# The opening of a pooling mixer, rebuilt: the scale row spread by TensorE, another load order, whole float32 weights for two tiles

## The chip, the cores and the metric

The kernel runs on one core of a Trainium2 chip. The metric is the device time of one execution in microseconds (us), as the median of several runs. The core has five engines, each with an instruction stream of its own that it works through in order: TensorE (PE, matrix products), VectorE (DVE), ScalarE (ACT), GpSimd (POOL) and SyncE (SP, which issues most DMAs). They wait for each other through semaphores.

## The reference: what is computed

One layer of a decoder trunk on x of 1024 tokens by 1024 channels, float32. The first half is the pooling mixer, the second a gated ConvFFN:

```python
h = rms_norm(x, norm_mix_g)
# per group of 256 channels, windows (2, 4, 8, 16):
d = causal_window_mean(h, w) - h
y = scale * (einsum('bsgc,gcd->bsgd', d, w) + b)
x = x + y
f = conv_ffn(rms_norm(x, norm_ffn_g))   # 1024 -> 2*2816, conv of 3, silu(gate)*val, 2816 -> 1024
x = x + f
```

`rms_norm` multiplies by the gain and by 1/sqrt(mean(x*x) + 1e-6).

## The kernel before, in words

The tokens are cut into eight tiles of 128 rows, `xs[0]` to `xs[7]`. A loop over j runs a software pipeline in which tile j is normed, tile j-1 is pooled, tile j-2 is multiplied by the mixer's weights and tile j-4 becomes an operand of the FFN. The steps of a tile:

- `rstd_of` (L127 to L138): ACT sums the squares of a tile (`junk`, L130) and takes a square root (L131); DVE then makes the reciprocal root from it with five operations on one column (`st`, L132 to L137). There is one such norm per tile ahead of the mixer (`st_a`), one ahead of the FFN (`st_b`), and one for `x_edge` (`st_e`).
- `mixer_norm` (L145): DVE multiplies the band matrix of the four windows by each row's reciprocal root (`bandr`, L147). The pooling is a matmul of the tile with that matrix, so the norm costs nothing more.
- `mixer_window` (L188): PE makes the pooled tile `psd` with eight float32 matmuls of 128 columns (L151; a record each for two halves, so x16 in the trace). DVE corrects the first 16 columns of each chunk: for tile 0 by a factor (L196), for the others by adding `edges`, what the window takes from the tile before (L198). ACT rounds the result to `dh` (L199), DVE makes the rest `dl` (L200).
- `mixer_edges` (L166): `x_edge` holds the last 16 rows of each of the first seven tiles (rows 16 to 127 of it). It has a norm of its own and an `edge_band`; PE makes `ps_edges` for all tiles at once, ACT copies it to `edges` (L169).
- `mixer_weights` (L175): DVE multiplies the weights `wp_raw` by the scale row, spread over 128 partitions, and by the norm's gain (L178); ACT rounds them to `wph` (L183), DVE makes the rest `wpl` (L184).
- `mixer_bias` (L157): the bias row, spread over 128 partitions too, times the scale, split in two parts for a matmul with a constant matrix (L159 to L162, L215).
- `mixer_out` (L206): PE multiplies, per chunk, dh*wph + dh*wpl + dl*wph, 24 matmuls of 256 columns (`psy`, L214), and two of 512 columns for the bias (L215). DVE adds the tile itself (L217), SP stores it (L218), and the second norm follows (`diag`, L221).
- `ffn_operand` (L233): PE transposes and norms the tile (`pst`, L237), ACT and DVE scale it into `n2f` and split it into operands of the FFN's matmuls.

The FFN (L263 to the end) is a Strassen-like scheme of three-term matmuls (L303, L576) whose weights come in as `win` tiles of 1 MB. Its first two, `win0` and `win1`, are loaded inside the mixer's loop, into the two buffers of the tag "raw" that `wp_raw` and `rows_b` (scale and bias rows) have held.

The order on each engine is fixed when the program is built: a scheduler places the instructions from the order of the code and from what they depend on, and `tc.issue_after(mark)` holds a group of instructions back behind a marked one. On an engine nothing overtakes. All loads of the opening are issued by SP, in the order of L108 to L119.

Of the kernel before, what the change touches and what calls it, by code (L numbers as in the profile page):

```python
# [7 lines left out]
F32 = mybir.dt.float32  # L8
F32R = mybir.dt.float32r
# [12 lines left out]
NG = 4  # L22
# [11 lines left out]
BD = B0 + NG * P  # L34

NOPS_A = 3
ACT_GAIN = 7

NH = 512
# [4 lines left out]
def trunk_kernel(ctx: ExitStack, tc: tile.TileContext, x, consts, par, rows, pool_w, w_in, w_out, out):  # L44
# [16 lines left out]
    def raw_tile(name):  # L61
        return work.tile([P, 2, D], F32, tag="raw", name=name, bufs=2)
# [24 lines left out]
    def affine(t, src, op, fill, base, pattern, step):  # L87
        nc.gpsimd.affine_select(out=t, in_=src, compare_op=op, fill=fill, base=base, pattern=pattern, channel_multiplier=step)

    nc.gpsimd.memset(x_edge[:HALO, :], 0.0)  # L90
    for g, w in enumerate(WINDOWS):

        e = edge_band[:, g, :].rearrange("p (j t) -> p j t", t=HALO)
        nc.gpsimd.memset(edge_band[:, g, :], 1.0 / w)
        affine(e, e, ALU.is_gt, 0.0, w - HALO, [[-HALO, NS], [-1, HALO]], 1)
        affine(e, e, ALU.is_ge, 0.0, HALO - 1, [[HALO, NS], [0, HALO]], -1)
    for g, w in enumerate(WINDOWS):

        m = band[:, g, :]
        nc.gpsimd.memset(m, 1.0 / w)  # L100
        affine(m, m, ALU.is_ge, 0.0, 0, [[1, P]], -1)
        affine(m, m, ALU.is_gt, 0.0, w, [[-1, P]], 1)
        affine(m, m, ALU.not_equal, 1.0 / w - 1.0, 0, [[1, P]], -1)
    par_sb = const.tile([P, NPAR], F32, tag="par", name="par_sb")
    wp_raw = raw_tile("wp_raw").rearrange("p a (c d) -> p (a c) d", d=GRP)
    rows_b = raw_tile("rows_b")
    scale_b, bias_b = rows_b[:, 0, :], rows_b[:, 1, :]
    load_x(0)  # L108
    nc.sync.dma_start(cst, consts)
    nc.sync.dma_start(x_edge[HALO:, :], x.rearrange("(j r) d -> j r d", r=P)[: NS - 1, P - HALO :, :])  # L110
    nc.sync.dma_start(par_sb, par)
    nc.sync.dma_start(scale_b, rows[:1, :].to_broadcast([P, D]))
    load_x(1)
    for g in range(0, NG, 2):
        nc.sync.dma_start(wp_raw[:, 2 * g : 2 * g + 4, :], pool_w[g : g + 2].rearrange("g (k p) d -> p (g k) d", p=P))
# [6 lines left out]
    nc.vector.memset(eps_t, EPS)  # L122
# [4 lines left out]
    def rstd_of(src, name):  # L127
        junk = pp.tile([P, D], BF16, tag="junk", name=f"junk_{name}")
        st = pp.tile([P, 4], F32, tag="st", name=f"st_{name}", bufs=8)
        nc.scalar.activation(junk, src, AF.Square, accum_out=st[:, 0:1])  # L130
        nc.scalar.activation(st[:, 1:2], st[:, 0:1], AF.Sqrt, bias=eps_t, scale=1.0 / D)  # L131
        nc.vector.tensor_scalar(st[:, 0:1], st[:, 0:1], 1.0 / D, EPS, op0=ALU.mult, op1=ALU.add)  # L132
        nc.vector.reciprocal(st[:, 2:3], st[:, 1:2])

        nc.vector.scalar_tensor_tensor(st[:, 3:4], st[:, 2:3], st[:, 0:1], st[:, 2:3], op0=ALU.mult, op1=ALU.mult)
        nc.vector.tensor_scalar(st[:, 3:4], st[:, 3:4], -0.5, 1.5, op0=ALU.mult, op1=ALU.add)
        nc.vector.tensor_tensor(st[:, 2:3], st[:, 2:3], st[:, 3:4], ALU.mult)  # L137
        return st[:, 2:3]  # L138

    bands, marks, stats = {}, {}, {}  # L140

    def edge_norm():
        nc.vector.tensor_scalar(edge_band, edge_band, rstd_of(x_edge, "e"), None, op0=ALU.mult)

    def mixer_norm(j):  # L145
        t = bands[j] = pp.tile([P, NG, P], F32, tag="bandr", name=f"bandr{j}", bufs=2)
        nc.vector.tensor_scalar(t, band if j else band0, stats[j], None, op0=ALU.mult)  # L147

    def windows(ps, src, weights):
        for c in range(NK):  # L150
            nc.tensor.matmul(ps[:, c * P : (c + 1) * P], src[:, c * P : (c + 1) * P], weights[:, c // 2, :], start=True, stop=True)  # L151


    bias_hl = pp.tile([P, D], F32R, tag="bias_hl", name="bias_hl")
    mean_w = pp.tile([P, P], F32R, tag="mean_w", name="mean_w")

    def mixer_bias():  # L157
        nc.vector.memset(mean_w.bitcast(F32), 2.0 / P)
        nc.vector.tensor_tensor(bias_b, bias_b, scale_b, ALU.mult)  # L159
        nc.scalar.activation(bias_hl, bias_b, AF.Copy)  # L160
        low = slice(P // 2, P)
        nc.vector.tensor_tensor(bias_hl[low, :], bias_b[low, :], bias_hl[low, :].bitcast(F32), ALU.subtract)  # L162

    edges = pp.tile([P, NK, P], F32, tag="edges", name="edges")

# [9 lines left out]
    def mixer_weights():  # L175
        for c in range(2 * NG):
            g = c // 2
            nc.vector.scalar_tensor_tensor(  # L178
                wp_raw[:, c, :], scale_b[:, g * GRP : (g + 1) * GRP], par_sb[:, GM + c : GM + c + 1], wp_raw[:, c, :], op0=ALU.mult, op1=ALU.mult
            )  # L180
            if c % 2:
                cs = slice(c - 1, c + 1)
                nc.scalar.activation(wph[:, cs, :], wp_raw[:, cs, :], AF.Copy)  # L183
                nc.vector.tensor_tensor(wpl[:, cs, :], wp_raw[:, cs, :], wph[:, cs, :].bitcast(F32), ALU.subtract)  # L184

    ds = {}

    def mixer_window(j):  # L188
        ps = bank2(f"psd{j}")
        windows(ps, xs[j], bands.pop(j))  # L190
        dh = pp.tile([P, NK, P], F32R, tag="dh", name=f"dh{j}", bufs=2)
        dl = pp.tile([P, NK, P], F32R, tag="dl", name=f"dl{j}", bufs=1)
        ps3 = ps.rearrange("p (c s) -> p c s", c=NK)
        first = ps3[:, :, :HALO]
        if j == 0:
            nc.vector.tensor_tensor(first, first, fac, ALU.mult)  # L196
        else:
            nc.vector.tensor_tensor(first, first, edges[:, :, j * HALO : (j + 1) * HALO], ALU.add)  # L198
        nc.scalar.activation(dh, ps3, AF.Copy)  # L199
        nc.vector.tensor_tensor(dl, ps3, dh.bitcast(F32), ALU.subtract)  # L200
        ds[j] = (dh, dl)

    n2s = {}
    x1_dram = dram.tile([S, D], F32, tag="x1_dram", name="x1_dram")

    def mixer_out(j):  # L206
        dh, dl = ds.pop(j)
        ps = bank2(f"psy{j}")
        for h in range(2):
            cols = slice(h * NH, (h + 1) * NH)  # L210
            for c in range(4 * h, 4 * h + 4):
                o = ps[:, c // 2 * GRP : (c // 2 + 1) * GRP]
                for i, (a, w) in enumerate(((dh, wph), (dh, wpl), (dl, wph))):
                    nc.tensor.matmul(o, a[:, c, :], w[:, c, :], start=c % 4 == 0 and i == 0, stop=False, skip_group_check=True)  # L214
            nc.tensor.matmul(ps[:, cols], mean_w, bias_hl[:, cols], start=False, stop=True, skip_group_check=True)  # L215
        x1 = xs.pop(j)
        marks[j] = nc.vector.tensor_tensor(x1, ps, x1, ALU.add).ins  # L217
# [3 lines left out]
        nc.vector.tensor_scalar(diag, ident, r, None, op0=ALU.mult)  # L221
        n2s[j] = (x1, diag)

    n2f = n2_pool.tile([P, NK, S], F32, tag="n2f", name="n2f")
# [164 lines left out]
    for j in range(NS + 4):  # L389
        if j < NS:  # L390
            mixer_norm(j)
        if j == 0:
            edge_norm()
            stat(1)
        if 0 <= j - 1 < NS:
            mixer_window(j - 1)
        if j == 1:
            mixer_edges()
            mixer_weights()
            mixer_bias()  # L400
# [12 lines left out]
        stat(j + 1)  # L413
# [191 lines left out]
def constants():  # L605

    import numpy as np

    r, t, h = np.arange(P)[:, None], np.arange(P), np.arange(HALO)
    blocks = [np.eye(P)]  # L610
    blocks += [np.tile(w / np.minimum(h + 1, w), (P, 2)) for w in WINDOWS]
    inside = [(r > t - w) & (r <= t) for w in WINDOWS]
    blocks += [(m - np.eye(P) * np.minimum(t + 1, w)) / w for m, w in zip(inside, WINDOWS)]
    return np.concatenate(blocks, axis=1).astype(np.float32)


# [32 lines left out]
```

## Time and profile before

| what | value |
|---|---|
| median of 3 runs | 720.9 us (719.9 to 721.37) |
| the profiled execution | 723.45 us |
| its span, first to last instruction | 721.7 us |
| granted TensorE clock over the span | 0.995 |
| PE busy | 698.9 us (97%) |
| DVE busy | 609.7 us (84%) |
| ACT busy | 352.3 us (49%) |

All rows of the trace are of the profiled execution, counted from the start of its span. A timeline row reads: start, duration, engine, line, operation, what it writes <- what it reads, partitions x elements, count, and in brackets the idle time just before it with what ended it. In a table of windows each engine has its busy time in the stretch with the number of instructions; then come the granted clock (1.00 is full), the DMA engines' busy share and the bytes they moved per second. SPq marks the issue of a DMA by SP: its duration is the time to issue, not to transfer.

### The profile page before, as it was taken

What the parts mean: (1) busy time and instruction counts of PE and PEld (TensorE: products, weight loads), DVE (VectorE), ACT (ScalarE), POOL (GpSimd) and SP (SyncE); (2) the same over time, 40 slices, a digit from 0 to 9 for tenths busy, and PEclk for the clock granted to TensorE, in tenths of its full rate; (3) what the DMA queues carried; (4) which work ended last, traced back from release to release, by engine and by line L of the source; (5) the groups of instructions that cost most, each with busy time, mean ns of one, the idle gap of its engine ahead of it and who ended that gap; (6) DMA issues with size and microseconds to landing.
All of it is one profiled execution on the core that took longest, in us unless ns stands there. A gap on an engine that the chain in (4) does not pass through costs nothing.

```text
span 721.7 us, 8803 instructions
## 1 busy us (share of the span) xinstructions
PE 698.9 (97%) x3252; PEld 580.2 (80%) x3252; DVE 609.7 (84%) x941; ACT 352.3 (49%) x566; POOL 7.7 (1%) x33
## 2 busy tenths in 40 slices
PE   3799999999999999999999999999999999999997
PEld 3799977888888888888888888888888788888886
DVE  3788999999888898888888888877996998798994
ACT  4597746554444444444444444444553444344441
POOL 4000000000000000000000000000000000000000
PEclk9899999999999999999999999999999999999999
DMA  9722030222222222222122112227999910005241
GB/s 266 282 89 84 34 117 0 118 88 88 88 87 88 88 88 89 87 88 81 66 89 73 58 75 87 88 89 264 315 321 312 308 54 1 0 1 190 87 152 67
DMA packets 30881, 83.83 MB, mean 116 GB/s; under 512 B 3335, under 2 KB 4487, under 8 KB 28023
## 3 DMA queue, kind: packets, MB, share of 16 engines
q1 hardware_dynamic: 30839, 83.28, 32.8%
q8 instruction: 25, 0.41, 0.2%
q14 instruction: 17, 0.14, 0.1%
HBM read 63.34 MB, written 19.92 MB: 115 GB/s over the span
## 4 chain that ended last, share of the span: by engine, by line
PE 80%; DVE 11%; DMA 6%; issue 1%; SPq 1%; ACT 1%; DVEq 0%; ACTq 0%
PE Y L303 23%; PE oP L576 21%; PE X L303 15%; PE Z L303 15%; PE psy L214 3%; DMA blk<-g_dram 3%; PE psd L151 2%; DMA x<-in_x_dram 1%; PE pst L237 1%; DVE n2f L271 1%; DVE oBP L70 1%; DVE T L260 1%; DMA blk<-in_w_out_dram 1%; DVE blk L271 1%; DVE oAP L70 1%
## 5 line engine op out<-in xcount | busy, mean ns | idle before, releaser
L576 PE MATMUL oP<-oBP,oAP 128*128 128x512 f32 x924 | 210.8, 390 | 1.0 <-ACT oBP L69 0.6
L576 PEld LDWEIGHTS oP<-oBP,oAP 128*128 128x128 f32 x924 | 173.2, 188 | 38.5 <-DVE oBP L70 1.4
L303 PE MATMUL X<-B,A11s 128*128 128x512 f32 x264 | 65.6, 394 | 0.7 <-DVE A11s L70 0.7
L303 PE MATMUL Y<-T,S2s 128*128 128x512 f32 x264 | 65.1, 394 | 1.1 <-DVE T L260 1.0
L303 PE MATMUL Z<-B,S4s 128*128 128x512 f32 x264 | 64.1, 392 | 0.6 <-DVE r L337 0.6
L303 PE MATMUL Z<-T,S1s 128*128 128x512 f32 x264 | 64.6, 393 | 0.0
L303 PE MATMUL Y<-T,S3s 128*128 128x512 f32 x264 | 64.3, 392 | 0.0
L303 PE MATMUL Y<-T,A22s 128*128 128x512 f32 x264 | 64.1, 392 | 0.0
L303 PE MATMUL X<-B,A12s 128*128 128x512 f32 x264 | 63.4, 390 | 0.0
L303 PEld LDWEIGHTS Y<-T,S2s 128*128 128x128 f32 x264 | 49.2, 188 | 13.2 <-DVE T L260 1.5
L303 PEld LDWEIGHTS X<-B,A11s 128*128 128x128 f32 x264 | 49.3, 188 | 12.3 <-DVE A11s L70 1.1
L303 PEld LDWEIGHTS Z<-B,S4s 128*128 128x128 f32 x264 | 49.5, 188 | 11.8 <-issue 1.1
L303 PEld LDWEIGHTS Z<-T,S1s 128*128 128x128 f32 x264 | 49.5, 188 | 11.4 <-ACT S1s L69 0.2
L303 PEld LDWEIGHTS Y<-T,S3s 128*128 128x128 f32 x264 | 49.6, 188 | 11.2
L303 PEld LDWEIGHTS Y<-T,A22s 128*128 128x128 f32 x264 | 49.5, 188 | 11.1 <-ACT val L350 0.3
L303 PEld LDWEIGHTS X<-B,A12s 128*128 128x128 f32 x264 | 49.5, 188 | 10.3
L361 ACT ACTIVATE gate<-gate 128x1024 f32<-128x1024 f32 x22 | 23.4, 1061 | 43.5 <-DVE gate L352 43.5
L69 ACT ACTIVATE oBP<-blk 128x512 fp32r<-128x512 f32 x32 | 20.2, 633 | 46.9 <-PE oP L576 41.6
L351 DVE SCALAR_TENSOR_TENSOR val<-ha,par_sb,val 128x1023 f32<-128x1023 f32 x22 | 28.2, 1282 | 12.5 <-ACT val L350 12.5
L343 DVE TENSOR_TENSOR ha<-Z,q 128x512 f32<-128x512 f32 x20 | 13.8, 691 | 23.9 <-PE Z L303 23.9
L69 ACT ACTIVATE S4s<-win 128x512 fp32r<-128x512 f32 x22 | 13.9, 633 | 40.4 <-PE Z L303 35.9
L350 ACT ACTIVATE gate<-hb,par_sb 128x1024 f32<-128x1024 f32 x22 | 27.4, 1245 | 11.9 <-DVE hb L345 11.9
(130 smaller groups left out, 1094.2 us busy)
## 6 DMA issues: line engine op xcount, KB each, us to landing
win<-in_w_in_dram SPq DMA_DIRECT2D x22, 1024.0 KB, 4.8
g_dram<-val SPq DMA_DIRECT2D x22, 512.0 KB, 2.6
blk<-g_dram SPq DMA_DIRECT2D x33, 256.0 KB, 5.4
blk<-in_w_out_dram SPq DMA_DIRECT2D x31, 256.0 KB, 5.5
A12s<-g_dram SPq DMA_DIRECT2D x22, 256.0 KB, 5.0
B21s<-in_w_out_dram SPq DMA_DIRECT2D x22, 256.0 KB, 3.5
x<-in_x_dram SPq DMA_DIRECT2D x8, 512.0 KB, 10.4
x_dram<-x SPq DMA_DIRECT2D x8, 512.0 KB, 2.6
```

Source lines behind the costliest of these rows:

```text
L69: nc.scalar.activation(t[:, 0, :], src, AF.Copy)
L70: nc.vector.tensor_tensor(t[:, 1, :], src, t[:, 0, :].bitcast(F32), ALU.subtract)
L151: nc.tensor.matmul(ps[:, c * P : (c + 1) * P], src[:, c * P : (c + 1) * P], weights[:, c // 2, :], start=True, stop=True)
L214: nc.tensor.matmul(o, a[:, c, :], w[:, c, :], start=c % 4 == 0 and i == 0, stop=False, skip_group_check=True)
L237: nc.tensor.matmul(ps[:, c * P : (c + 1) * P], x1[:, c * P : (c + 1) * P], diag, start=True, stop=True)
L271: nc.vector.tensor_tensor(out, a, b, ALU.subtract)
L303: nc.tensor.matmul(bank, a[:, i, ks], b[:, l, k, :], start=opens and m == 0, stop=m == 11, skip_group_check=not opens)
L343: tt(hid[n, "a"][:, NH:], bank, hid[n, "q2"], ALU.add)
L350: nc.scalar.activation(t, src, AF.Identity, bias=par_sb[:, CB + f : CB + f + 1], scale=w[2])
L351: nc.vector.scalar_tensor_tensor(t[:, 1:], src[:, : S - 1], w[1], t[:, 1:], op0=ALU.mult, op1=ALU.add)
L361: nc.scalar.activation(gate, gate, AF.Silu)
L576: nc.tensor.matmul(obanks[set_, i], a[:, u, i * P : (i + 1) * P], b[:, v, :], start=opens and g == 0 and m == 0, stop=g == NP2 - 1 and m = ...
```

## The change

It has five parts, all in the mixer's opening.

1. **Rows.** The scale row and the bias row are no longer broadcast by two DMAs of 512 KB. The scale row is loaded once into one partition (4 KB), and PE spreads it with two float32 matmuls of one row of ones (`scale`, 512 columns each); DVE's weight scaling reads it from PSUM. Both rows are loaded as 8 partitions of 128 (`rows8`); the bias is multiplied and split there and two DMAs of 4 KB, issued by ACT, lay it out as two rows (`bias_hl`), so that the bias matmul has a contraction of 2 rows.
2. **Load order.** x of tile 0, rows, constants, parameters, weights, `x_edge`, tiles 1 to 7.
3. **Whole weights.** Tiles 0 and 1 (`WHOLE = 2`) are multiplied in plain float32, eight matmuls of 256 columns, with `wp_raw` and an unrounded `dh`; no `dl`. The split of the weights is held back behind the band of tile 1 and the copy of tile 0. `mixer_out(0)` stands before `mixer_edges` now.
4. **Norm.** Three operations instead of five on one column, and two factors where the norm is applied; the constants take a factor `FOLD` for it.
5. **Table.** A square root of one column (`warm`) at the start makes ACT load the table of the square root first.

```diff
     load_x(0)
+    nc.sync.dma_start(row_sb, rows[:1, :])
+    nc.sync.dma_start(rows8, rows.rearrange("r (k p) -> k r p", p=P))
     nc.sync.dma_start(cst, consts)
-    nc.sync.dma_start(x_edge[HALO:, :], x.rearrange("(j r) d -> j r d", r=P)[: NS - 1, P - HALO :, :])
     nc.sync.dma_start(par_sb, par)
-    nc.sync.dma_start(scale_b, rows[:1, :].to_broadcast([P, D]))
-    load_x(1)
+
     for g in range(0, NG, 2):
         nc.sync.dma_start(wp_raw[:, 2 * g : 2 * g + 4, :], pool_w[g : g + 2].rearrange("g (k p) d -> p (g k) d", p=P))
-    load_x(2)
-    nc.sync.dma_start(bias_b, rows[1:, :].to_broadcast([P, D]))
-    for j in range(3, NS):
+    nc.sync.dma_start(x_edge[HALO:, :], x.rearrange("(j r) d -> j r d", r=P)[: NS - 1, P - HALO :, :])
+    for j in range(1, NS):
         load_x(j)
...
+    warm = pp.tile([P, 1], F32, tag="warm", name="warm")
+    nc.scalar.activation(warm, eps_t, AF.Sqrt)
...
-        nc.scalar.activation(st[:, 1:2], st[:, 0:1], AF.Sqrt, bias=eps_t, scale=1.0 / D)
-        nc.vector.tensor_scalar(st[:, 0:1], st[:, 0:1], 1.0 / D, EPS, op0=ALU.mult, op1=ALU.add)
-        nc.vector.reciprocal(st[:, 2:3], st[:, 1:2])
-
-        nc.vector.scalar_tensor_tensor(st[:, 3:4], st[:, 2:3], st[:, 0:1], st[:, 2:3], op0=ALU.mult, op1=ALU.mult)
-        nc.vector.tensor_scalar(st[:, 3:4], st[:, 3:4], -0.5, 1.5, op0=ALU.mult, op1=ALU.add)
-        nc.vector.tensor_tensor(st[:, 2:3], st[:, 2:3], st[:, 3:4], ALU.mult)
-        return st[:, 2:3]
+        nc.scalar.activation(st[:, 1:2], st[:, 0:1], AF.Sqrt, bias=eps_t)
+        nc.vector.tensor_scalar(st[:, 0:1], st[:, 0:1], D * EPS, None, op0=ALU.add)
+
+        nc.vector.scalar_tensor_tensor(st[:, 3:4], st[:, 1:2], st[:, 1:2], st[:, 0:1], op0=ALU.mult, op1=ALU.add)
+        nc.vector.reciprocal(st[:, 2:3], st[:, 3:4])
+        return st[:, 1:2], st[:, 2:3]
...
+    ones = pp.tile([2, P], F32R, tag="ones", name="ones")
+    nc.vector.memset(ones.bitcast(F32), 1.0)
+    scale_b = []
+    for h in range(2):
+        t = ps_x.tile([P, NH], F32, tag="X", name=f"scale{h}")
+        nc.tensor.matmul(t, ones[:1, :].bitcast(F32), row_sb[:, h * NH : (h + 1) * NH], start=True, stop=True)
+        scale_b += [t[:, :GRP], t[:, GRP:]]
...
     def mixer_bias():
+        b = rows8[:, 1, :]
+        nc.vector.tensor_tensor(b, b, rows8[:, 0, :], ALU.mult)
+        nc.scalar.activation(bias8[:, 0, :], b, AF.Copy)
+        nc.vector.tensor_tensor(bias8[:, 1, :], b, bias8[:, 0, :].bitcast(F32), ALU.subtract)
+        for l in range(2):
+            nc.scalar.dma_start(bias_hl[l : l + 1, :].bitcast(F32), bias8[:, l, :].bitcast(F32))
...
+        if j < WHOLE:
+            dh = dh.bitcast(F32)
+            marks[f"whole{j}"] = nc.scalar.activation(dh, ps3, AF.Copy).ins
+            ds[j] = [(dh, wp_raw)]
+            return
...
+        if j == 0:
+            mixer_bias()
+            mixer_weights(range(4))
         if j == 1:
+            with tc.issue_after(marks["first"]):
+                mixer_weights(range(4, 8))
+            mixer_out(0)
             mixer_edges()
-            mixer_weights()
-            mixer_bias()
-        if 0 <= j - 2 < NS:
+        if 1 <= j - 2 < NS:
             mixer_out(j - 2)
+        if j == 2:
+            with tc.issue_after(marks["band1"]), tc.issue_after(marks["whole0"]):
+                split_weights()
```

Two places of the order show what moved. The first is SP's, from the start of the program; `x_122` is tile 0, and in the program before `x_128`, `x_132` and `x_135` are tiles 1 to 3, in the changed one `x_131`, `x_133` and `x_135`. Before:

```order
L81 DMA x_122<-in_x_dram 128x1024
L109 DMA cst<-in_consts_dram 128x768
L110 DMA x_edge<-in_x_dram 112x1x1024
L111 DMA par_sb<-in_par_dram 128x192
L112 DMA rows_b<-in_rows_dram 128x1024
L81 DMA x_128<-in_x_dram 128x1024
L115 DMA wp_raw<-in_pool_w_dram 128x4x256 x2
L81 DMA x_132<-in_x_dram 128x1024
L117 DMA rows_b<-in_rows_dram 128x1024
L81 DMA x_135<-in_x_dram 128x1024
```

And changed:

```order
L85 DMA x_122<-in_x_dram 128x1024
L115 DMA rows_raw<-in_rows_dram 1x1024
L116 DMA rows_raw<-in_rows_dram 8x2x128
L117 DMA cst<-in_consts_dram 128x768
L118 DMA par_sb<-in_par_dram 128x192
L121 DMA wp_raw<-in_pool_w_dram 128x4x256 x2
L122 DMA x_edge<-in_x_dram 112x1x1024
L85 DMA x_131<-in_x_dram 128x1024
L85 DMA x_133<-in_x_dram 128x1024
```

`x_edge` has moved from third to behind both loads of the weights, and tile 1 behind it; the two loads of 128x1024 from the rows are gone.

The second place is ACT's, from its first work on `x_edge`. Suffixes tell the tiles apart: `junk_a_200` and `st_a_201` are the norm of tile 1 before, `junk_a_209` that of tile 2, `dh_229` tile 0. Before:

```order
L130 ACTIVATE junk_e,st_e<-x_edge 128x1024
L131 ACTIVATE st_e<-st_e,eps_t 128x1
L130 ACTIVATE junk_a_200,st_a_201<-x_128 128x1024
L131 ACTIVATE st_a_201<-st_a_201,eps_t 128x1
L199 ACTIVATE dh_229<-psd_220 128x1024
L183 ACTIVATE wph<-wp_raw 128x512
L169 ACTIVATE edges<-ps_edges 128x1024
L130 ACTIVATE junk_a_209,st_a_210<-x_132 128x1024
```

And changed, where `junk_a_203` is tile 1, `junk_a_219` tile 2, `junk_b_257` the second norm of tile 0 and `junk_a_276` tile 3:

```order
L216 ACTIVATE dh_237<-psd_228 128x1024
L137 ACTIVATE junk_e,st_e<-x_edge 128x1024
L199 ACTIVATE wph<-wp_raw 128x512
L138 ACTIVATE st_e<-st_e,eps_t 128x1
L137 ACTIVATE junk_a_203,st_a_204<-x_131 128x1024
L199 ACTIVATE wph<-wp_raw 128x512
L138 ACTIVATE st_a_204<-st_a_204,eps_t 128x1
L137 ACTIVATE junk_a_219,st_a_220<-x_133 128x1024
L199 ACTIVATE wph<-wp_raw 128x512
L138 ACTIVATE st_a_220<-st_a_220,eps_t 128x1
L199 ACTIVATE wph<-wp_raw 128x512
L137 ACTIVATE junk_b_257,st_b_258<-x_122 128x1024
```

The copy of tile 0 (`dh`) has moved ahead of the work on `x_edge`, a rounding of the weights stands between each sum of squares and its root, and the copy `edges` has moved behind the second norm of tile 0. On PE the changed program begins with the two `scale` matmuls and `psd` of tile 0; then come `psy` of tile 0, `ps_edges`, `psd` of tiles 1 and 2, `psy` of tile 1, `psd` of tile 3, `psy` of tile 2, and from there the same rows as before.

More of the change, by code (lines that the diff above doesn't have):

```diff
@@ L26 @@
 EPS = 1e-6
+FOLD = 2 * D**0.5
 CW, CB, GM = 0, 3 * 2 * NF, 4 * 2 * NF
@@ L36 @@
 NOPS_A = 3
+WHOLE = 2
 ACT_GAIN = 7
@@ L93, in trunk_kernel @@
         e = edge_band[:, g, :].rearrange("p (j t) -> p j t", t=HALO)
-        nc.gpsimd.memset(edge_band[:, g, :], 1.0 / w)
+        nc.gpsimd.memset(edge_band[:, g, :], FOLD / w)
         affine(e, e, ALU.is_gt, 0.0, w - HALO, [[-HALO, NS], [-1, HALO]], 1)
@@ L173, in trunk_kernel, with mixer_weights, split_weights @@
     wpl = pp.tile([P, 2 * NG, GRP], F32R, tag="wpl", name="wpl")
-    def mixer_weights():
-        for c in range(2 * NG):
-            g = c // 2
+    def mixer_weights(cs):
+        for c in cs:
             nc.vector.scalar_tensor_tensor(
-                wp_raw[:, c, :], scale_b[:, g * GRP : (g + 1) * GRP], par_sb[:, GM + c : GM + c + 1], wp_raw[:, c, :], op0=ALU.mult, op1=ALU.mult
+                wp_raw[:, c, :], scale_b[c // 2], par_sb[:, GM + c : GM + c + 1], wp_raw[:, c, :], op0=ALU.mult, op1=ALU.mult
             )
[L181 to L184, printed above, removed]
+    def split_weights():
+        for c in range(0, 2 * NG, 2):
+            cs = slice(c, c + 2)
+            nc.scalar.activation(wph[:, cs, :], wp_raw[:, cs, :], AF.Copy)
+            nc.vector.tensor_tensor(wpl[:, cs, :], wp_raw[:, cs, :], wph[:, cs, :].bitcast(F32), ALU.subtract)
     ds = {}
```

44 lines of the change are left out of this document (21 added, 23 removed).

## The prediction, made before the changed kernel ran

> **What bounds the kernel now.** I read the page's head first, then a table of windows over the whole program.
>
> ```profile
> span 721.7 us, 8803 instructions
> PE 698.9 (97%) x3252; PEld 580.2 (80%) x3252; DVE 609.7 (84%) x941; ACT 352.3 (49%) x566; POOL 7.7 (1%) x33
> ...
> 0.00:35.00 35.00, 19.54 (x117) 18.23 (x118) 17.62 (x53) 18.20 (x30) 7.68 (x33) 0.90 0.85 282
> 35.00:75.70 40.70, 40.70 (x331) 39.66 (x330) 35.17 (x104) 33.43 (x84) 0.00 (x0) 1.00 0.20 79
> 75.70:112.00 36.30, 33.91 (x172) 27.81 (x171) 36.25 (x57) 23.27 (x48) 0.00 (x0) 1.00 0.20 73
> 112.00:600.00 488.00, 486.94 (x2120) 397.52 (x2121) 424.36 (x575) 230.06 (x324) 0.00 (x0) 1.00 0.34 121
> ```
>
> The columns after the stretch are PE, PEld, DVE, ACT and POOL. From 35 to 75.7 us PE is busy all the time, while DVE has 5.5 us to spare and ACT 7.3. From 75.7 to 112 DVE is (36.25 of 36.30): the FFN's first operands. After that it is PE again. Only the first 35 us are bound by none: there PE works 19.54 us and waits for the rest. An edit in the opening is worth what it brings forward the point from which PE never waits again. All that follows moves with that point, as long as its own bound does the same work. The timeline of PE shows it:
>
> ```profile
> 8.66 3.40 PE L151 MATMUL psd<-bandr,x 128*128 128x128 f32 x16 [8.66 <-DVE bandr L147]
> 14.42 3.35 PE L151 MATMUL ps_edges<-edge_band,x_edge 128*128 128x128 f32 x16 [2.36 <-DVE edge_band L143]
> 18.81 2.05 PE L151 MATMUL psd<-bandr,x 128*128 128x128 f32 x16 [1.04 <-DVE bandr L147]
> ...
> 25.22 2.93 PE L151 MATMUL psd<-bandr,x 128*128 128x128 f32 x12 [2.66 <-DVE bandr L147]
> ...
> 31.46 0.39 PE L214 MATMUL psy<-wph,dh 128*128 128x256 f32 x1 [0.71 <-DVE dl L200]
> ...
> 34.91 1.95 PE L151 MATMUL psd<-bandr,x 128*128 128x128 f32 x16
> ```
>
> The last row is the pooling of tile 3. From there both programs have the same PE rows in the same order (pooling of 3, product of 2, transpose of 0, pooling of 4). So I follow the changed program to that point and compare it with 34.91.
>
> **The loads.** What the first tiles wait for is DMA. From the timeline of SP, the table of DMA issues (its last column is us to landing), the answer on the tile `wp_raw`, and two windows:
>
> ```profile
> 1.25 0.42 SPq L109 DMA_DIRECT2D cst<-in_consts_dram  x1
> ...
> cst<-in_consts_dram SPq DMA_DIRECT2D x1, 384.0 KB, 4.0
> L115 SPq DMA_DIRECT2D wp_raw<-in_pool_w_dram x2: 434/714/995, 4.1 to 4.6; - x2
> ...
> DMA to landing us min/median/max: 11.4/11.9/12.4
> ...
> 5.00:11.00 6.00, 2.34 (x11) 2.34 (x12) 1.47 (x6) 1.94 (x4) 3.32 (x15) 1.00 1.00 177
> 11.00:23.00 12.00, 8.14 (x51) 7.24 (x50) 8.88 (x31) 8.99 (x17) 0.00 (x0) 0.86 1.04 392
> ```
>
> And from the timeline of ACT:
>
> ```profile
> 4.21 1.06 ACT L130 ACTIVATE junk_a<-x 128x1024 bf16<-128x1024 f32 x1 [2.13 <-DMA x<-in_x_dram]
> ...
> 5.38 1.28 ACT L131 ACT_TABLE_LOAD   x1
> 6.67 0.29 ACT L131 ACTIVATE st_a<-st_a,eps_t 128x1 f32<-128x1 f32 x1
> 11.40 1.06 ACT L130 ACTIVATE junk_e<-x_edge 128x1024 bf16<-128x1024 f32 x1 [4.44 <-DMA x_edge<-in_x_dram]
> ...
> 14.06 1.06 ACT L130 ACTIVATE junk_a<-x 128x1024 bf16<-128x1024 f32 x1 [1.18 <-DMA x<-in_x_dram]
> ...
> 15.44 1.00 ACT L199 ACTIVATE dh<-psd 128x1024 fp32r<-128x1024 f32 x1
> ...
> 18.73 1.05 ACT L130 ACTIVATE junk_a<-x 128x1024 bf16<-128x1024 f32 x1
> ...
> 19.78 0.63 ACT L183 ACTIVATE wph<-wp_raw 128x512 fp32r<-128x512 f32 x1
> 20.32 0.28 ACT L131 ACTIVATE st_a<-st_a,eps_t 128x1 f32<-128x1 f32 x1
> 20.57 0.63 ACT L183 ACTIVATE wph<-wp_raw 128x512 fp32r<-128x512 f32 x1
> ```
>
> The constants, second in the queue, land at 1.25 + 4.0 = 5.25. `x_edge`, next in it, is there at 11.40: 6.1 us for 448 KB, and through all of it the DMA engines are busy (share 1.00) but move 177 GB/s, against 392 before and after they are rid of it. The slow stretch goes with `x_edge`: the second broadcast lies in the fast one, so a broadcast is not slow by itself. I take 6.1 us as the price of this transfer wherever it stands.
>
> In the changed order 96 KB of parameters and 1 MB of weights go ahead of it. At 392 GB/s that is 2.9 us. The two halves of the weights landed 1.5 us apart (11.4 and 12.4 after issues at 4.1 and 4.6), so 3.0 us and 0.3 for the parameters is as good: the weights are there at 8.5, `x_edge` at 14.6, 3.2 us later than now. Tile 1 follows 1.3 us (512 KB at 392) behind, 15.9 (now 14.06, when its norm starts), tile 2 at 17.2, tile 3 at 18.6. The 1 MB of broadcasts that goes is in these.
>
> **Before `x_edge` matters.** The rows that price it on DVE:
>
> ```profile
> 7.00 0.15 DVE L132 TENSOR_SCALAR st_a<-st_a 128x1 f32<-128x1 f32 x1 [5.90 <-ACT st_a L131]
> ...
> 8.12 0.49 DVE L147 TENSOR_SCALAR bandr<-cst,st_a 128x512 f32<-128x512 f32 x1
> 12.91 0.15 DVE L132 TENSOR_SCALAR st_e<-st_e 128x1 f32<-128x1 f32 x1 [4.31 <-ACT st_e L131]
> ...
> 13.88 0.49 DVE L143 TENSOR_SCALAR edge_band<-edge_band,st_e 128x512 f32<-128x512 f32 x1
> 14.28 0.29 DVE L196 TENSOR_TENSOR psd<-psd,cst 128x128 f32<-128x128 f32 x1
> ...
> 15.71 0.47 DVE L178 SCALAR_TENSOR_TENSOR wp_raw<-rows_b,par_sb,wp_raw 128x256 f32<-128x256 f32 x1
> ...
> 18.67 0.68 DVE L184 TENSOR_TENSOR wpl<-wp_raw,wph 128x512 fp32r<-128x512 f32 x1
> ...
> 31.33 1.21 DVE L217 TENSOR_TENSOR x<-psy,x 128x1024 f32<-128x1024 f32 x1
> ```
>
> Tile 0's root comes 1.3 us sooner, since the table load at 5.38 goes: 5.4 to 5.7. Five small operations took 0.97 us (12.91 to 13.88), three take 0.6. The bias' two DVE operations stand ahead of `bandr`, and the second waits for ACT's copy between them, with `bandr` queued behind it: three operations on 128 columns, at most 0.3 each (L196), 0.8 with handovers. So `bandr` ends at 5.7 + 0.6 + 0.8 + 0.5 = 7.6.
>
> PE meanwhile spreads the scale row: 128 float32 columns cost 0.425 in the cold row (8 matmuls in 3.40), 512 cost 1.7, the two 3.4, from 4.3 (the row lies behind tile 0, which landed at 4.2) to 7.7; at the warm rate of the 18.81 row half that. Neither end delays `psd` of tile 0 by more than 0.1. It takes 1.8 to 3.4 and ends at 9.5 to 11.1; halo 0.3, copy 1.0 (L199), product from 10.9 to 12.5.
>
> The whole product is eight float32 matmuls of 256 columns: twice the columns of a `psd`, so about 3.6, and the bias:
>
> ```profile
> 36.86 1.43 PE psy L214 x12
> 38.28 0.23 PE psy L215
> ```
>
> These two rows, from the chain of waits, are half a three-term product: 3.3 in all. The whole one is 3.6 + 0.46 = 4.0, 0.7 dearer on PE, and needs neither `dl` (1.2 on DVE) nor the split. It ends at 14.9 to 16.5; the weights' scaling (8 x 0.40, in two blocks) is done at 11.7. All of this has cover until `edge_band`, at 17.6; cold throughout, it would cost some 0.7.
>
> The bias' 4 KB DMAs are not in the trace: issued at 7.3, needed at 13. The quickest landing above is 4.0, the slowest 12.4: 11.3 to 19.7. I take the quick one, which costs nothing, as they are small and in ACT's own queue; the slow one holds `psy` of tile 0 to 21.9 and moves the end 2.4 later.
>
> **From `x_edge` on.** ACT takes 1.05 from a sum of squares to the rounding behind it, 0.54 to the root, 0.25 to the next start (18.73, 19.78, 20.32, 20.57): 1.84 for each norm with its share of the split. `junk_e` starts at 14.6, its root ends at 16.5; tile 1's root at 18.3, tile 2's at 20.2. On DVE `edge_band` is made from 17.1 to 17.6 and PE does the edges from 17.65, cold again after more than 2 us of idling (the 14.42 row): 3.35, to 21.0. `bandr` of tile 1 is there at 19.4; then come tile 0's sum (1.2, to 20.6) and, woven into tile 2's norm, three subtractions of the split (0.68 each), so tile 2's `bandr` is there only at 23.2. PE: `psd` of tile 1 from 21.0 to 22.8, of tile 2 from 23.2 to 25.0.
>
> ACT, behind the split: second norm of tile 0 (20.7), copy of the edges (21.7 to 22.7), squares of tile 3 (22.9), `dh` of tile 1 at 24.0 to 25.0. So tile 1's whole product runs from 25.0 to 29.0, and `psd` of tile 3 starts at 29.0, against 34.91: 5.9 us sooner. Tile 3's `bandr` (26.1) and `dl` of tile 2 (28.3) are earlier than their use.
>
> Behind that PE is full as before. The norms take less of DVE, which was not late there. In the stretch that DVE bounds, tile 7's norm saves two operations of at most 0.15: 0.2. Sum: **6.1 us**. The profiled execution took 723.45 (span 721.7 and 1.75 around it), so it would take 717.3; it stood 2.55 above the median of 720.9, which becomes **714.8**.
>
> **Rivals.**
>
> *`x_edge` is quick by itself* and was slow because it ran beside the first broadcast, which is gone. For it: both began in the slow stretch. Against: the other broadcast shows 392. At 392 GB/s it takes 1.2 us, to 9.7. Then ACT itself, free at 11.2 after `dh` of tile 0, sets the chain, and all of it is 14.6 - 11.2 = 3.4 us earlier: 711.4. [...]
>
> *ACT waits for `win1`.*
>
> ```profile
> DMA to landing us min/median/max: 4.8/6.1/7.4
> ```
>
> This is the row of `win`. `win1` takes the buffer of `wp_raw`, which the whole product of tile 1 reads until 29.0; it lands at 33.8 to 36.4. ACT reaches its split at about 33.4 (`psd` of tile 3 ends at 30.8, halo and `dh` at 32.1, then a root and the squares of tile 5), with tile 5's root and the copies of `pst` behind it. Most of at most 3.0 us lies in ACT's spare 7.3; I price the rest at 1.0: 715.8.
>
> *Slower: `x_edge` gets later still.* It ran beside a broadcast and tile 1; now tiles 1 to 4 are queued right behind it. Every norm stands behind `junk_e` on ACT, so each microsecond of it is one of the total. The gain is gone when it lands at 14.6 + 6.1 = 20.7: if it shared the 177 GB/s with more than three tiles and ended with them (12.2 us are 2.16 MB, of which 0.46 are its own). With four it would land at 22.9 and the time would be 723.1. Against it: in the trace it was there at 11.40, well before tile 1 (14.06), which was queued behind it.
>
> *The change doesn't do what it says*: the order shows that it does; the point at which PE stops waiting could still be set by another wait, and the first row to show that is `dh` of tile 1.
>
> **Numbers.** Forecast 0.60, quick `x_edge` 0.22, `win1` 0.11, slow 0.07 (of which 0.03 end slower, 0.03 within 0.2%). 0.2% is 1.4 us, about what a measurement of this kernel tells from no change. The range runs from 710.5 (the quick case less 0.9 for the spread of the runs) to 717.5 (the bias' slow landing, 717.2). Faster 0.94, same 0.03, slower 0.03.
>
> **What would show it.** `junk_e` starting at about 14.6, its idle time ended by the DMA of `x_edge`; 177 GB/s in 8.5 to 14.6; PE on `ps_edges` at 17.6 and on `psd` of tile 3 at 29.0; DVE full from about 70 to 106. The first step is wrong if `junk_e` starts by 12 (then 711) or after 17; the sum is wrong if `psd` of tile 3 starts at 29 but PE has gaps before 70, or if DVE's full stretch grows beyond 36 us.

## The result, and the profile after

The changed kernel is slower: 725.48 us (median of 5 runs, 725.27 to 727.22) against 721.37 (5 runs, 719.9 to 722.43), ratio 1.0063, 95% interval 1.0045 to 1.0082. Forecast was 714.8. The profiled execution took 726.2 us, span 724.5 (before: 723.45, span 721.7).

The opening first. From the timelines of ACT and of PE in the changed kernel (start, duration, engine, line; the bracket holds the idle time ahead of the row and what ended it):

```profile
16.30 1.06 ACT L137 ACTIVATE junk_e<-x_edge 128x1024 bf16<-128x1024 f32 x1 [3.16 <-DMA x_edge<-in_x_dram]
```

```profile
16.44 0.49 PE L236 MATMUL psy<-bias_hl,ones 2*128 2x512 f32 x1 [1.25 <-DMA bias_hl<-rows_raw]
...
19.50 2.05 PE L159 MATMUL ps_edges<-edge_band,x_edge 128*128 128x128 f32 x16 [0.22 <-DVE edge_band L146]
...
24.94 2.02 PE L159 MATMUL psd<-bandr,x 128*128 128x128 f32 x16 [1.60 <-issue]
26.80 1.89 PE L235 MATMUL psy<-wp_raw,dh 128*128 128x256 f32 x8
28.62 0.49 PE L236 MATMUL psy<-bias_hl,ones 2*128 2x512 f32 x1
```

And the chain of waits behind that, two halves of tile 2, the transpose of tile 0 and the pooling of tile 4, and so on:

```profile
31.46 1.98 PE psd L159 x16
33.44 1.42 PE psy L235 x12
34.86 0.42 PE psy L236
35.28 1.63 PE psy L235 x12
36.91 0.42 PE psy L236
37.33 1.98 PE pst L258 x16
39.31 1.79 PE psd L159 x16
...
46.98 1.79 PE psd L159 x16
```

The pooling of tile 3 starts at 31.4 instead of 34.91: against that execution the opening did gain 3.5 us. Then look at L236, the bias: 0.42 each, where the kernel before had 0.23, and the group behind each is 0.2 longer as well (1.63 against 1.44 for the same twelve matmuls, 1.98 against 1.78 for `pst`). From one pooling to the next it is 7.67 us (6.90 in the chain of the kernel before). Three more places show what became of the 3.5 us. PE's timeline before, at the last transpose, at a product that waits for DVE in the stretch which it bounds, and at the first and last products of the FFN's second half:

```profile
81.90 1.95 PE L237 MATMUL pst<-diag,x 128*128 128x128 f32 x16
...
102.67 5.08 PE L303 MATMUL Y<-T,S2s 128*128 128x512 f32 x21 [1.05 <-DVE T L260]
...
505.97 4.29 PE L576 MATMUL oP<-oBP,oAP 128*128 128x512 f32 x18
...
713.81 4.01 PE L576 MATMUL oP<-oBP,oAP 128*128 128x512 f32 x17
```

And after:

```profile
82.99 1.95 PE L258 MATMUL pst<-diag,x 128*128 128x128 f32 x16
...
103.56 5.10 PE L324 MATMUL Y<-T,S2s 128*128 128x512 f32 x21 [0.59 <-DVE T L281]
...
506.87 3.39 PE L604 MATMUL oP<-oBP,oAP 128*128 128x512 f32 x14
...
713.68 6.91 PE L604 MATMUL oP<-oBP,oAP 128*128 128x512 f32 x29
```

A lead of 3.5 at tile 3 is a lag of 1.1 at the last transpose: 4.6 us went in the mixer's steady part, where 12 bias matmuls lie. The lag is 0.9 behind DVE's stretch and stays so for 400 us. In the last stage it grows once more, from 0.9 to 2.8 (717.82 against 720.59).

### The profile page after: what moved, and what is told of

It reads as the page before. It is cut to its first block, busy times and chain, and to the rows that moved or that the text cites. A ratio compares the mean times of both kernels' runs of the same rounds, so it can differ in the third digit from the quotient of the medians.

```text
span 724.5 us, 8744 instructions
## 1 busy us (share of the span) xinstructions
PE 707.4 (98%) x3240; PEld 579.2 (80%) x3240; DVE 605.8 (84%) x905; ACT 350.4 (48%) x566; POOL 8.2 (1%) x33
## 4 chain that ended last, share of the span: by engine, by line
PE 80%; DVE 8%; DMA 8%; issue 1%; SPq 1%; ACT 1%; DVEq 0%; ACTq 0%
PE Y L324 23%; PE oP L604 21%; PE X L324 15%; PE Z L324 14%; PE psy L235 3%; DMA blk<-g_dram 3%; PE psd L159 2%; DMA x_edge<-in_x_dram 2%; PE pst L258 1%; DMA blk<-in_w_out_dram 1%; DVE T L281 1%; SPq L509 1%; DVE n2f L292 1%; PE psy L236 1%; DVE oBP L74 1%
## 5 line engine op out<-in xcount | busy, mean ns | idle before, releaser
L324 PEld LDWEIGHTS X<-B,A11s 128*128 128x128 f32 x264 | 49.3, 188 | 12.2 <-DVE A11s L74 1.1
L324 PEld LDWEIGHTS Y<-T,S3s 128*128 128x128 f32 x264 | 49.6, 188 | 11.2
```

Source lines behind the costliest of these rows:

```text
L324: nc.tensor.matmul(bank, a[:, i, ks], b[:, l, k, :], start=opens and m == 0, stop=m == 11, skip_group_check=not opens)
```

## The experiments

The theory after the result: the opening gained, and the bias matmul with a contraction of 2 rows costs 0.38 us more each, 0.19 of its own and 0.19 at the matmul behind it. The rivals: the late `x_edge` or the whole weights ate the gain, or a later stage did. No run tests the parts 4 (norm) and 5 (table) alone. Where no other median stands beside a run, that of the kernel before in the same series was 721.9 to 722.8.

**The bias over 128 rows.** `bias128` is the changed kernel with

```diff
-    ones = pp.tile([2, P], F32R, tag="ones", name="ones")
+    ones = pp.tile([P, P], F32R, tag="ones", name="ones")
-    bias_hl = pp.tile([2, D], F32R, tag="bias_hl", name="bias_hl")
+    bias_hl = pp.tile([P, D], F32R, tag="bias_hl", name="bias_hl")
+    nc.vector.memset(bias_hl.bitcast(F32), 0.0)
```

> The changed kernel with the bias matmul over 128 rows (rows 2 to 127 are zeros, written once by DVE at the start). Theory, the two-row matmul: each of the 12 bias matmuls behind the pooling of tile 3 costs 0.23 us again instead of 0.42 and its neighbour 1.43 instead of 1.63, 4.6 us less in all, about 720.5 us, a little below the kernel before; period of a tile 6.9 us instead of 7.67. Rival, the late x_edge or the later stages lose the gain: the matmul's shape changes nothing, 725 us.

Measured: 721.51 us, ratio to before 0.9981 (0.9965 to 0.9996), so 4 us under the change (4.7 when each is counted from the median of the kernel before beside it). The chain of `bias128`:

```profile
34.11 1.44 PE psy L236 x12
35.54 0.23 PE psy L237
35.77 1.44 PE psy L236 x12
37.22 0.23 PE psy L237
37.45 1.78 PE pst L259 x16
39.23 1.79 PE psd L159 x16
...
46.14 1.79 PE psd L159 x16
```

From pooling to pooling it is 6.91 us again. That is the theory's size, 0.76 a tile. And the lead at tile 3 is no longer lost: 2.75 us there against the 34.91 of the kernel before, 2.63 at the last transpose against its 81.90.

```profile
32.16 1.95 PE L159 MATMUL psd<-bandr,x 128*128 128x128 f32 x16
...
79.27 1.95 PE L259 MATMUL pst<-diag,x 128*128 128x128 f32 x16
```

What makes the difference is in the timeline of the weight loads (PEld), the kernel after first:

```profile
34.47 0.19 PEld L235 LDWEIGHTS psy<-wph,dl 128*128 128x128 f32 x1
34.79 0.18 PEld L236 LDWEIGHTS psy<-bias_hl,ones 2*128 2x128 f32 x1
35.21 0.19 PEld L235 LDWEIGHTS psy<-wph,dh 128*128 128x128 f32 x1 [0.24 <-issue]
```

The same place in `bias128`:

```profile
35.14 0.19 PEld L236 LDWEIGHTS psy<-wph,dl 128*128 128x128 f32 x1
35.26 0.19 PEld L237 LDWEIGHTS psy<-bias_hl,ones 128*128 128x128 f32 x1
35.38 0.19 PEld L236 LDWEIGHTS psy<-wph,dh 128*128 128x128 f32 x1
35.62 0.19 PEld L236 LDWEIGHTS psy<-wpl,dh 128*128 128x128 f32 x1
```

With 128 rows a load of 0.19 us starts every 0.12 us, so that each overlaps the one ahead of it, and the weights of the next matmul are in (35.38 + 0.19 = 35.57) before the bias matmul is through (35.77 in the chain). With 2 rows the load comes 0.32 after the one ahead of it, and the next 0.42 later still. Two loads of 0.18 and 0.19 us laid open would make 0.37 of the 0.38; that is an estimate from these rows: that the loads are laid open, and what would keep them so, no run shows.

**The 2 rows alone, in the kernel before.** `before_bias2` multiplies two rows of the bias' high part by 0.5 and leaves its low part out:

```diff
-        nc.vector.memset(mean_w.bitcast(F32), 2.0 / P)
+        nc.vector.memset(mean_w.bitcast(F32), 0.5)
-            nc.tensor.matmul(ps[:, cols], mean_w, bias_hl[:, cols], ...)
+            nc.tensor.matmul(ps[:, cols], mean_w[:2, :], bias_hl[:2, cols], ...)
```

> The kernel before with a bias matmul of two rows alone (the low part of the bias is left out). Theory, the two-row matmul: 16 matmuls by 0.38 us, of which two to four lie in the waits of the opening: 4.6 to 6.1 us slower than before, 726 to 727.5 us. Rival: as before, 721.4 us, since all of the loss comes from other parts of the change.

Measured: 730.76 us, ratio 1.0121 (1.0102 to 1.0139), 8.7 us slower than the 722.06 beside it. The direction is the theory's, the size beyond its 6.1. Behind tile 3 the 12 matmuls cost what they should (7.87 us later than the kernel before at the last transpose, 4.6 more than at tile 3); the pooling of tile 3 itself was 3.2 us later than 34.91, since PE waited 2.6 us for `bias_hl` with the first bias matmul and then ran slow:

```profile
25.32 0.79 PE L215 MATMUL psy<-bias_hl,mean_w 2*128 2x512 f32 x1 [2.62 <-ACT bias_hl L160]
...
29.61 3.78 PE L151 MATMUL psd<-bandr,x 128*128 128x128 f32 x16
```

In the kernel before, the pooling of tile 2 stood in this wait; here it came behind the product. So this run bears the theory out but does not measure it cleanly.

**How many rows.** `bias32` and `bias64` are `bias128` with 32 and 64 rows.

> The bias matmul over 32 rows (30 of zeros). If every matmul with fewer than 128 rows between full ones loses the load of its weights beside the matmul ahead of it: 0.42 us for each, 725 us as with two rows. If only less than a quarter of the array does: 0.23 us and 720.5 us.

> The changed kernel with the bias over 64 rows. If any matmul on fewer than 128 rows between full ones costs 0.38 more with its neighbour: 490 ns in the table as with 2 and 32 rows. If half of the rows is enough: 390 to 400 as with 128.

Measured: 726.15 us, ratio 1.0056 (1.0039 to 1.0074), and 725.72 in one run. The groups by form (busy us, mean ns of one), `bias32`:

```profile
L237 PE MATMUL psy<-bias_hl,ones 32*128 32x512 f32 x16 | 7.8, 490 | 0.0
```

`bias64`, and the kernel after:

```profile
L237 PE MATMUL psy<-bias_hl,ones 64*128 64x512 f32 x16 | 7.9, 492 | 0.4 <-DMA bias_hl<-rows_raw 0.4
```

```profile
L236 PE MATMUL psy<-bias_hl,ones 2*128 2x512 f32 x16 | 7.8, 490 | 1.3 <-DMA bias_hl<-rows_raw 1.3
```

2, 32 and 64 rows cost the same. The groups' means aren't set against that of `bias128`, 462, since four of the 16 stand in the opening among float32 products and slow rows; in the steady part a row takes 0.49 us with 2, 32 or 64 rows and 0.39 to 0.40 with 128, the two bias matmuls of a tile start 2.04 us apart (34.13 and 36.17 in `bias32`, 34.88 and 36.92 in `bias64`, 34.80 and 36.84 in the kernel after) against 1.67 in `bias128` (35.38 and 37.05), and from pooling to pooling it is 7.67 us in `bias32`. So it is not a price for very few rows: half of them cost as much. Whether a stream of equal small matmuls would pay it, no run shows.

**Why `x_edge` is slow.** `bias128_xe7` loads it by seven DMAs of 16 rows, on top of `bias128`:

```diff
-    nc.sync.dma_start(x_edge[HALO:, :], x.rearrange("(j r) d -> j r d", r=P)[: NS - 1, P - HALO :, :])
+    for j in range(1, NS):
+        nc.sync.dma_start(x_edge[j * HALO : (j + 1) * HALO, :], x[j * P - HALO : j * P, :])
```

> The bias over 128 rows, and x_edge loaded by seven DMAs of 16 rows instead of one of 7 x 16 rows. Theory, the one DMA is slow because it is laid on 7 of the 16 DMA engines: x_edge lands at about 11 us instead of 16.3, the squares of it start at 11.5 or as soon as ACT is free, and the end comes 3 to 4 us sooner than with bias128 alone, about 717 us. Rival, its rows of 4 KB far apart are slow in themselves, or the queue: x_edge lands at about 16 again and the time is that of bias128, 720.5 us.

Measured: 721.18 us, ratio 0.9985 (0.9973 to 0.9997): no gain over `bias128`. But the run doesn't answer the question. Nothing was whole at 11 us, as the theory had it: the last of the seven was issued only at 12.0. `x_edge` no longer held ACT, but with six issues more the program's order on DVE came out another, and the edges' norm was put behind tile 0's sum, which waited for PE:

```profile
18.93 1.23 DVE L240 TENSOR_TENSOR x<-psy,x 128x1024 f32<-128x1024 f32 x1 [5.26 <-PE psy L238]
20.07 0.14 DVE L140 TENSOR_SCALAR st_e<-st_e 128x1 f32<-128x1 f32 x1
```

`bias128_r16` keeps every instruction and its place, and turns the two loops of the one DMA:

```diff
-    nc.sync.dma_start(x_edge[HALO:, :], x.rearrange("(j r) d -> j r d", r=P)[: NS - 1, P - HALO :, :])
+    nc.sync.dma_start(x_edge[HALO:, :], x.rearrange("(j r) d -> r j d", r=P)[P - HALO :, : NS - 1, :])
```

> As the kernel with the bias over 128 rows, but x_edge in one DMA whose outer loop runs over the 16 rows of a block and the inner over the 7 blocks (its rows then lie in another order than edge_band has them, which changes the halo's values and no instruction). Same bytes, same rows of 4 KB, same issue. Theory, 7 of 16 DMA engines make it slow: it lands at 11 to 12 us instead of 16 to 17.7, the squares of it start at 13 at the latest, the pooling of tile 3 at 28.5 to 29.5 instead of 32.2, and the time is about 3 us under bias128, 718.5. Rival, the rows or their place in the queue: lands at 16 again, 721.5.

Measured: 718.39 us, ratio 0.9923 (0.9894 to 0.9952). From its timelines of ACT and PE:

```profile
12.12 1.02 ACT L217 ACTIVATE dh<-psd 128x1024 f32<-128x1024 f32 x1 [5.11 <-DVE psd L212]
13.04 1.05 ACT L137 ACTIVATE junk_e<-x_edge 128x1024 bf16<-128x1024 f32 x1
```

```profile
29.12 1.95 PE L159 MATMUL psd<-bandr,x 128*128 128x128 f32 x16
```

ACT doesn't wait for `x_edge` at all now. Bandwidth from 11 to 14 us (last column), in the kernel after and in `bias128_r16`:

```profile
11.00:14.00 3.00, 1.55 (x8) 1.18 (x8) 1.86 (x5) 1.02 (x1) 0.00 (x0) 1.00 1.01 202
```

```profile
11.00:14.00 3.00, 1.55 (x6) 1.17 (x6) 1.86 (x5) 1.89 (x3) 0.00 (x0) 1.00 1.01 362
```

The busy share is 1.01 in both and doesn't tell them apart; the rate does, 202 GB/s against 362. The same turn in the kernel before, `before_r16`:

> The kernel before with x_edge alone changed to the loop order of 16 rows outside and 7 blocks inside (its halo values come out in another order than edge_band has them). Theory, the shape of the one DMA sets its time: it lands at 7 to 9 us instead of 10.4 to 11.4, tile 1 behind it 2 us sooner too, and the pooling of tile 3 comes 2 to 3 us sooner, at 30 to 32; time 719 to 720. Rival, the first broadcast beside it makes it slow, whatever its shape: 10.4 again and time as before.

Measured: 720.44 us, ratio 0.9971 (0.9957 to 0.9984), 1.7 us under the 722.1 beside it. `x_edge` landed at 8.0 (issue at 1.7, 6.3 to landing):

```profile
8.07 1.06 ACT L130 ACTIVATE junk_e<-x_edge 128x1024 bf16<-128x1024 f32 x1 [1.16 <-POOL band L88]
```

The pooling of tile 3 started at 31.82. So the shape of the one DMA makes the slow stretch, in either place and beside a broadcast or not. As for the 7 of 16 engines in the theories, no row names the engines that carry a transfer; what the traces keep, though no row above prints it, is each raise of a transfer's semaphore. When `x_edge` landed there were seven raises in the kernel before (11.04 to 11.32) and seven in the change (13.96 to 16.22), but sixteen in `bias128_r16` (10.01 to 12.24) and sixteen in `before_r16` (6.38 to 7.99), as for the load of tile 0 in all four (3.71 to 4.19 in the kernel before). So seven against sixteen is shown for the raises; for the engines it stays the author's reading.

From the constants to `x_edge` 6.1 us passed in the kernel before, from the weights to it 5.4 in the change. The raises show that seven parts of what is queued behind it come only with it: of the parameters' sixteen in the kernel before, nine came by 6.17 and seven from 11.30 to 11.50, 8.8 us after the issue. In the change, where the parameters go ahead of `x_edge`, they took 4.4.

**What is left of the opening.** `best` is `bias128_r16` with `edge_band` in the same order, as 512 more columns of constants:

```diff
+    nc.sync.dma_start(edge_band, consts[:, BD:].rearrange("p (g s) -> p g s", s=P))
+    nc.sync.dma_start(x_edge[HALO:, :], x.rearrange("(j r) d -> r j d", r=P)[P - HALO :, : NS - 1, :])
```

and without the 12 operations of GpSimd that made it, so that the halo's values are right again; `best_whole1` sets `WHOLE = 1` besides.

> The changed kernel with three edits: the bias over 128 rows, x_edge in one DMA with 16 rows as its outer loop, and edge_band in that same order, loaded as 256 KB of constants ahead of x_edge (0.65 us at 392 GB/s) instead of built by GpSimd. It computes all that the reference does. Theory: pooling of tile 3 at 29.1 to 29.8 as with the other order of x_edge alone (29.12), the time 718 to 719, 3 to 5 us under the kernel before and about 7 under the change. Rival: the 256 KB more in the queue push x_edge behind ACT's copy of tile 0 (13.0) and cost 1 to 2 us: 720.

> The kernel of three edits, with whole float32 weights for tile 0 alone; tile 1 is split as the others are. Theory, the whole product of tile 1 saves its wait for dl and costs 0.6 more on PE (3.9 against 3.3): pooling of tile 3 within 0.5 us of where it was, time the same. Rival, the whole product is where the change loses: pooling of tile 3 0.6 us sooner or more, time 0.6 to 1 us shorter.

Measured: 719.01 us, ratio 0.9956 (0.9938 to 0.9973), and 717.71, ratio 0.9949 (0.9932 to 0.9967). The pooling of tile 3 in the two:

```profile
28.27 1.95 PE L154 MATMUL psd<-bandr,x 128*128 128x128 f32 x16
```

```profile
28.83 1.39 PE L154 MATMUL psd<-bandr,x 128*128 128x128 f32 x11
```

Both beat both kernels. The whole product of tile 1 brings 0.56 us at this point; between the two times the runs can't tell. So, measured on `best`, it is not what made the change slow.

**The opening of the kernel before differs from run to run.** `before_again` is that kernel unchanged; `before_dma2` adds two DMAs of 256 bytes on ACT's queue; `before_warm` gives PE idle work in its waits; `before_flip` moves `win` and the blocks behind it to the other buffer of their pair:

```diff
# before_dma2
+    for i in range(2):
+        nc.scalar.dma_start(tiny[i % 2 : i % 2 + 1, :], rows[i % 2 : i % 2 + 1, :64])
# before_warm: 20 of these ahead of the first pooling, 2 and 1 float32 ones behind psd0 and ps_edges, 8 in psy0
+            nc.tensor.matmul(fbank, w, by, start=True, stop=True)
# before_flip, ahead of win0
+            nc.vector.memset(raw_tile("spare")[:1, 0, :1], 0.0)
```

> The kernel before, unchanged: a second profile of it. If the slow clock of its opening (granted 0.90 up to 35 us, time 723.45 against a median of 721 to 722) belongs to that one execution: clock 1.0, the pooling of tile 3 one to three us before 34.91 and the time 720.5 to 721.5. If it is the rule: 34.9 again.

> The kernel before with two DMAs of 256 bytes more, issued by ACT at the start, as the change adds two for the bias; nothing reads what they bring. Theory, every transfer behind them changes its place among the DMA's semaphores, and the last stage (FFN's second product, 506 to 718 us; 211.9 us before, 213.7 after) gets longer by that: its stage takes 213.5 to 214.3 and the time is 1.8 to 2.4 us longer. Rival, the last stage differs by chance from one execution to the next: the time is that of before.

> The kernel before with idle work for PE in the waits of the opening (31 matmuls on constants and on tiles that stand there already, result unread), so that PE is never idle for 2 us. Theory, half of what the change brings in the opening is the clock: pooling of the edges 2.05 us instead of 3.35, of tile 2 without the slow 2.93, the pooling of tile 3 at 32.4 to 33 instead of 34.91, and the median 1 to 2 us under that of before. Rival, the waits for bands set the opening: the pooling of tile 3 at 34.5 or later, time as before.

> The kernel before with one empty tile taken from the buffers of win ahead of win0, so that all later tiles of that pair (win, and the first two blocks of the last stage) lie in the other buffer of the two, as they do in the changed kernel; one operation of one element more, all else in the same order. Theory, the place in SBUF makes the last stage (506 to 718 us) longer: 212.6 to 214.3 us of it as in all kernels built on the change, instead of 211.2 to 211.9 as in all built on the one before, and the time 1 to 2.5 us longer. Rival: 211.5, time as before.

Measured, `before_again`: 722.05 us, pooling of tile 3 at 34.11, which is neither of its two answers: 0.8 sooner, with `x_edge` at 10.40 instead of 11.40, and the clock granted up to 35 us was 0.95 instead of 0.90, not 1.0. `before_dma2`: 723.47, ratio 1.0005 (0.9986 to 1.0023); its profiled run took only 720.36, with that pooling at

```profile
32.35 1.95 PE L154 MATMUL psd<-bandr,x 128*128 128x128 f32 x16
```

`before_flip`: 722.18, ratio 1.0018 (0.9999 to 1.0038), 33.02. `before_warm`: 721.72, ratio 0.9982 (0.9967 to 0.9997), 33.81, which misses the 32.4 to 33 of its theory: PE still had a wait of 2.5 us ahead of tile 1 and a slow row of 3.05 behind it. Keeping PE busier is worth about 0.2% here, with an interval that comes close to nothing. What the four share is that 34.91, on which the prediction counted, was the latest of all: the kernel before, alone or with two DMAs or one tiny operation more, reaches that row between 32.35 and 34.91.

**The last stage.** From its first product to its last it took 211.9 us in the profile before and 213.7 after. The two theories of a cause, two more DMAs and another buffer, both fell: 211.2 in `before_dma2` and 211.0 in `before_flip`. Two more profiles of the change:

> The changed kernel once more, unchanged. If the longer last stage belongs to this kernel: 213.2 us or more from 506 to the end of its products, and the bias matmul 490 ns in any case. If it is chance: 211 to 212 in this profile or the other.

> The changed kernel a third time, unchanged, with the same two answers: 213.2 us or more in the last stage, or 211 to 212.

Measured: 726.1 and 725.86 us, last stage 213.8 and 213.7, so it does belong to the changed kernel. But kernels with the same order of instructions there took 214.3 (`bias128`), 212.9 (`bias128_r16`), 212.1 (`best`) and 210.7 (`best_whole1`), and `before_r16`, with the order of the kernel before, 214.1. The page's row of the products has 2.2 us idle (before 1.0), which is 1.1 of the 1.9:

```profile
L604 PE MATMUL oP<-oBP,oAP 128*128 128x512 f32 x924 | 211.5, 390 | 2.2 <-ACT oBP L73 1.1
```

Product for product, the lag grows between 550 and 568 us and nowhere else in the stage. It is 0.9 at the first product and 2.7 at these two, before and after, where PE waits for ACT:

```profile
561.16 0.49 PE L576 MATMUL oP<-oBP,oAP 128*128 128x512 f32 x1 [0.58 <-ACT oBP L69]
```

```profile
563.84 0.50 PE L604 MATMUL oP<-oBP,oAP 128*128 128x512 f32 x1 [1.10 <-ACT oBP L73]
```

In both traces ACT itself has just waited for a block that DMA brings (`A12s`, 3.2 and 3.3 us). What makes these transfers come up to 2 us later in some kernels is open.

## Why the prediction was wrong

The forecast missed by 725.48 - 714.8 = 10.7 us. By its own steps:

- **The step that failed** is "The whole one is 3.6 + 0.46 = 4.0" with "Behind that PE is full as before". The 0.46 are two matmuls from the row `38.28 0.23 PE psy L215`, of 128 rows; the change makes them matmuls of 2 rows, as its own description says, and the working doesn't ask what that costs. It is an omitted term: 0.38 us for each. PE was full, as forecast (35.00 us busy of the 35 from 35 to 70), but with dearer work. Behind tile 3 that is 12 x 0.385 = 4.6 (from +3.5 to -1.1), and tile 1's product took 4.6 instead of 4.0, another 0.6. `bias128` shows it: 4 us back from this edit alone, and tile 1's product back at 3.9. With 128 rows the change is faster by 0.2% (ratio 0.9981): the sign of the forecast right, its size not.
- **`x_edge` at 14.6**: the mechanism was right, the size not. It landed at 16.3, 1.7 later, and at 15.6 to 17.7 in the other kernels that load it so. The term that was off is the weights ahead of it: the second half was there at 10.9 (issued at 3.3, 7.6 to landing) and not at 8.5, since 288 GB/s moved from 5 to 11 us where the sum took 392; `x_edge` came 5.4 behind it, not 6.1. In `bias128_r16` that half landed at 10.7, so the loops of `x_edge` are not the reason; what is, no run tested. With `bandr` of tile 2 that made the pooling of tile 2 start at 24.9 instead of 23.2, and with the 0.6 above that of tile 3 at 31.4 instead of 29.0. The rival of a quick `x_edge` had its cause wrong (not the broadcast beside it, but the transfer's own shape) and its gain too high: freed of the wait, `best` reached tile 3 at 28.3, where the rival had 25.6; 1.8 of that is tile 0's copy, which ended only at 13.0 and not at 11.2.
- **The bias' DMAs** landed at 16.4, between the two bounds and nearer the slow one that was not taken. They held tile 0's product by 1.25 us, which `x_edge` covered: behind that product PE still waited 0.2 for `edge_band`. `ps_edges` took 2.05, not the cold 3.35, so PE finished it at 21.4, close to the 21.0 forecast: two errors, 1.9 late and 1.3 quick, met by luck. (The scale row's "half" at the warm rate is 0.6 by the rows, 2.05 against 3.40; it was spread at the slow rate in any case, 3.75 us for the two matmuls, and nothing hung on it.)
- **The norm's 0.2** in DVE's stretch came out by size, as the lag falls from 1.1 to 0.9 there, but it isn't shown: `bias128` has the same norm and gained nothing in that stretch (a lead of 2.63 at the last transpose, 2.62 at the FFN's second product). No run tested it alone.
- **The last stage** was taken as unchanged; it is 1.9 longer, cause open.
- **The step from span to median** cost 1.8. The profile before stood 2.55 above the median and I moved that whole surplus on to the changed kernel, whose profile stood only 0.7 above its own. Part of the surplus lay in the very stretch that the change replaces: 34.91 was a late execution. Against the other four profiles above (32.35 to 34.11) the opening gained 1.0 to 2.7 us, not 3.5.

In sum 2.4 (opening) + 4.6 (bias) + 1.9 (last stage) + 1.8 (median) = 10.7. No rival named the bias matmul; the slow rival, `x_edge` at 22.9, did not happen, and for `win1` ACT waited 0.38 us.

## What to carry to other kernels

A price from a row holds for the row's shape: when an edit changes the partition count of a matmul in a stream of full ones, take its cost as unknown, count how often it runs, and estimate it by a weight load on each side (0.18 and 0.19 us here, where the cost was 0.38 in all, 12 times where nothing covers it); zeros up to the full number of rows were cheaper here than fewer rows (721.51 us against 725.48). A stretch in which the DMA share is full at half the rate of other stretches (here 1.00 at 177 GB/s, against 392) is a reason to look at the outer loop of the DMA in it before that DMA is moved in the queue. And a gain in a stretch that varies between executions is counted against several of them (here that point came at 32.35 to 34.91), not against the one that was profiled.

## What the runs showed of the hardware

- A matmul of 2 rows among matmuls of 128 took 0.42 instead of 0.23 us in the chain, and the group behind it 0.19 to 0.20 more (`after`); with 32 and 64 rows its row took 0.49 us as with 2 (`bias32`, `bias64`); with 128 rows, 126 of them zeros, it took 0.23 again (`bias128`).
- One DMA of 448 KB with 7 blocks outside and 16 rows inside landed, in the changed place, at 15.6 to 17.7 us, with seven raises of its semaphore, and all engines together moved 202 GB/s from 11 to 14 us; with the loops turned it landed at 12.2, with sixteen, and they moved 362.
- Two DMAs of 4 KB from SBUF to SBUF, issued on ACT's queue at 7.0 and 8.3 while the loads ran (DMA share 1.0 from 5 to 14 us), had landed at 16.4, eight us after the second issue; in `best`, with the loops of `x_edge` turned, PE used them at 14.7 without a wait.
